# A decoder layer on one core: w_ada sums moved to TensorE, triangular inverses built from 16-blocks, and half the tokens' chunk work begun only with the first FFN

## The chip, the cores and the metric

The kernel runs on one core of a Trainium2 chip. A core has five engines that run side by side, each with its own instructions in a fixed order: TensorE (PE, matmuls, with PEld for its weight loads), VectorE (DVE), ScalarE (ACT), GpSimd (POOL) and SyncE (SP), which here issues nearly all transfers. The metric is the device time of one execution in microseconds (us).

## What is computed

One layer of a conditioned trunk, cut to what matters here (batch 1, 1024 tokens, width 1024, FFN width 2816):

```python
ada = silu(c) @ w_ada + b_ada                    # 1024 -> 6 x 1024
sh_m, sc_m, g_m, sh_f, sc_f, g_f = split(ada, 6)
h = rms_norm(x) * (1 + sc_m) + sh_m
z, u = split(h @ w_in)
y = concat(rwkv7_time_mix(shift(z)), s5_mix(u))  # 8 heads of 64; 32 groups of 16
x = x + g_m * (y @ w_out)
h = rms_norm(x) * (1 + sc_f) + sh_f
x = x + g_f * ((silu(h @ w_gate) * (h @ w_up)) @ w_down)
out = rms_norm(x) * final_gain
```

`rwkv7_time_mix` is a recurrence over tokens. The kernel does it in chunks, and each chunk needs the inverse of a unit triangular matrix.

## The kernel before

**Order.** The program is written as generators that are stepped in turn. `weave` steps several of them in proportion, `LIM(g, n)` takes n steps, `alongside(g, other, n)` runs `g` and takes a step of `other` after every n of its own. This sets priorities; a scheduler then fixes the order of each engine's instructions when the program is built. On the chip each engine takes them strictly in that order.

**Stages.** The start sums parts 0 and 1 of w_ada, normalises x and projects `u`. Then come the S5 work, the projection to z (`pz`) and the chunk work of four token quarters `qt` of 256 tokens. For each quarter `prepare` (tiles `pn`, `pa`, `pw`, `pb`, `pA`, `ak`) builds the chunk matrices, `post` inverts them, `chains` (tiles `p`, `R`, `U`, `ST`) runs the recurrence, and `finishes` (`pd`, `pv`, `pg`, `ld`) normalises, gates and writes y to the DRAM tensor `y_d`. `s5_glu` (`pglu`, `pss`, `zz`) is the S5 gate in four halves. `outproj(half)` reads y (`yt`, split in two parts `yhl`), loads w_out (`wraw`, `wo`) and forms `po`; `norm_f` and `ffn(half)` (`pgate`, `pup`, `pdn`) follow. Half 0 is quarters 0 and 1, half 1 quarters 2 and 3. `late` is the sequence of all the chunk work of quarters 2 and 3, 128 steps.

**w_ada.** `ada_load` (L280) loads 1024 rows of some columns in four tiles `wada`. `ada_acc` (L289) multiplies each of the eight row blocks by a column of silu(c), `cact`, and adds them up in `acc`: on DVE (L295, L297), or, for the first column pair of parts 2 and 3, with ACT multiplying (L299) and POOL adding (L300). `ada_cols` (L303) sums `acc` over partitions with one-column matmuls `pac`. `ada_steps` (L826) does this for two parts, 256 columns at a time: parts 2 and 3 along with the S5 gate and the chains, parts 4 and 5 with the first output projection.

**The inverse.** `solve` (L991) takes 32x32 blocks `LU` from DRAM and eliminates them in 31 steps of two instructions (`stmp` L1006, `XU` L1008), on DVE for quarters 0 and 1, on POOL for quarters 2 and 3. Result and transpose go to the DRAM tensor `x_d` and come back in another layout in `rest` (L1013), where `pG` and `pO` (32x32 tiles of PE) join two 32-blocks to a 64-block.

**The end of the program** (L1415 on) sets where `late` runs: 4 of its steps along with the first steps of the first output projection, 16 more along with the rest of it, and the others in `alongside(late, f0, 2)` (L1442): a step of `f0` after every two of `late`, where `f0` is `norm_f(0)` and `ffn(0)`, 97 steps. After it `f0` runs 28 steps alone, and what is left of it is woven with the second output projection.

## Time and profile before

| | |
|---|---|
| median of 3 runs | 1596.32 us (1594.2 to 1597.29) |
| profiled execution, its own time | 1596.48 us |
| its span in the profile | 1594.8 us |
| mean granted TensorE clock | 0.946 of 2.4 GHz |
| PE / DVE / ACT / POOL busy | 1419.0 / 929.3 / 562.7 / 519.8 us |
| first `pz` / first `pglu` / first `po` | 104.4 / 462.1 / 597.7 us |
| first `pgate` of FFN(0) / first `po` of half 1 / last `po` | 694.2 / 1115.2 / 1203.4 us |

Times in the trace count from the start of the span. An engine's busy share says little by itself, since the kernel passes through stages with different limits: what bounds a stage is read from that stage's windows and waits.

### The profile page before, as it was taken

Reading aid. Unit: us, or ns where it says so; the run is one execution under the profiler, and the core shown is the slowest. Engines: PE = TensorE matmul, PEld = TensorE weight load, DVE = VectorE, ACT = ScalarE, POOL = GpSimd, SP = SyncE. Lnnn points to the kernel's source line nnn. Section 1 sums busy time; section 2 is a strip of 40 time slices with the busy share of each in tenths; the row PEclk is TensorE's granted clock in tenths of the full one; section 3 lists DMA queues with packets and bytes.
Section 4 is the critical chain, followed back from the end, with each engine's and each line's share of the span. In section 5 each row is a group of like instructions: output and inputs, shape, how many; then the busy total and the mean of one; then the engine's idle time right before and its main releaser. Section 6 shows DMA issues by size and latency. Waiting matters only on the chain.

```text
span 1594.8 us, 23226 instructions
## 1 busy us (share of the span) xinstructions
PE 1419.0 (89%) x9167; PEld 1143.2 (72%) x9167; DVE 929.3 (58%) x1618; ACT 562.7 (35%) x909; POOL 519.8 (33%) x480
## 2 busy tenths in 40 slices
...
GB/s 286 139 139 244 264 328 193 164 163 110 154 160 125 126 219 217 59 103 97 61 99 91 88 106 89 84 54 167 177 80 40 151 87 106 92 106 92 98 101 53
DMA packets 255692, 211.80 MB, mean 133 GB/s; under 512 B 71894, under 2 KB 223072, under 8 KB 252000
## 3 DMA queue, kind: packets, MB, share of 16 engines
...
## 4 chain that ended last, share of the span: by engine, by line
PE 51%; DVE 19%; DMA 13%; POOL 5%; ACT 5%; issue 4%; SPq 2%; DVEq 0%; ACTq 0%; POOLq 0%
PE pdn L270 11%; PE pgate L270 10%; PE pup L270 10%; PE pz L270 5%; PE po L1314 4%; DMA wada<-in_w_ada_dram 3%; PE pu L367 2%; DMA rawd<-in_ffn_w_down_dram 2%; PE p L1062 2%; DVE acc L297 2%; POOL stmp L1006 2%; POOL XU L1008 2%; PE pY L762 1%; PE pA L962 1%; DMA LU<-l_d 1%
## 5 line engine op out<-in xcount | busy, mean ns | idle before, releaser
L270 PE MATMUL pdn<-wd,act 128*128 128x512 f32 x1056 | 271.7, 398 | 1.4 <-DVE x L1363 0.5
L270 PE MATMUL pup<-h,hl_up 128*128 128x512 f32 x1056 | 266.5, 395 | 0.2 <-ACT hl_up L131 0.2
L270 PE MATMUL pgate<-h,hl_g 128*128 128x512 f32 x1056 | 262.7, 394 | 2.1 <-ACT hl_g L131 2.0
L270 PEld LDWEIGHTS pdn<-wd,act 128*128 128x128 f32 x1056 | 197.3, 189 | 49.1 <-DVE x L1363 2.4
L270 PEld LDWEIGHTS pgate<-h,hl_g 128*128 128x128 f32 x1056 | 196.6, 188 | 47.2 <-issue 3.2
L270 PEld LDWEIGHTS pup<-h,hl_up 128*128 128x128 f32 x1056 | 197.5, 188 | 43.9 <-issue 2.1
L270 PE MATMUL pz<-hT,hl_z 128*128 128x256 f32 (+1 forms) x1008 | 192.6, 347 | 35.0 <-ACT zo L872 13.5
L1363 DVE TENSOR_TENSOR x<-pdn,x 128x512 f32<-128x512 f32 x176 | 118.8, 688 | 176.6 <-PE pdn L270 176.4
L270 PEld LDWEIGHTS pz<-hT,hl_z 128*128 128x128 f32 x1008 | 159.0, 206 | 64.8 <-ACT zo L872 18.2
L1398 DVE TENSOR_TENSOR rawd<-rawd,gfb 128x1024 f32<-128x1024 f32 x44 | 57.2, 1300 | 111.5 <-DMA rawd<-in_ffn_w_down_dram 89.9
L1314 PE MATMUL po<-wo,yhl 128*128 128x512 f32 x384 | 98.7, 410 | 9.0 <-ACT yhl L1299 4.2
L1314 PEld LDWEIGHTS po<-wo,yhl 128*128 128x128 f32 x384 | 74.4, 197 | 27.3 <-ACT yhl L1299 4.3
L131 ACT CAST wd<-rawd 128x1024 fp32r<-128x1024 f32 x44 | 45.6, 1051 | 122.1 <-DVE rawd L1398 88.8
L131 ACT CAST hl_up<-raw_up 128x1024 fp32r<-128x1024 f32 x44 | 46.2, 1051 | 114.6 <-PE pup L270 105.1
L297 DVE SCALAR_TENSOR_TENSOR acc<-wada,cact,acc 128x256 f32<-128x256 f32 (+1 forms) x112 | 79.0, 710 | 6.9 <-DMA wada<-in_w_ada_dram 5.3
L875 POOL TENSOR_TENSOR zo<-zo,zm 128x512 f32<-128x512 f32 x28 | 44.2, 1580 | 99.5 <-ACT zo L872 86.6
L127 POOL TENSOR_TENSOR hl_g<-raw_g,hl_g 128x1024 fp32r<-128x1024 f32 x19 | 45.5, 2394 | 78.7 <-ACT hl_g L131 78.7
L127 POOL TENSOR_TENSOR yhl<-yt,yhl 128x512 fp32r<-128x512 f32 x16 | 25.0, 1562 | 135.5 <-ACT yhl L1299 130.9
L1392 ACT ACTIVATE sgt<-pgate 128x512 f32<-128x512 f32 x44 | 26.3, 599 | 121.0 <-PE pgate L270 120.0
L127 POOL TENSOR_TENSOR wd<-rawd,wd 128x1024 fp32r<-128x1024 f32 x19 | 49.7, 2616 | 57.4 <-ACT wd L131 57.4
L127 POOL TENSOR_TENSOR wo<-wraw,wo 128x512 fp32r<-128x512 f32 x32 | 44.4, 1393 | 73.6 <-ACT wo L131 73.6
L127 POOL TENSOR_TENSOR hl_up<-raw_up,hl_up 128x1024 fp32r<-128x1024 f32 x19 | 49.9, 2628 | 50.0 <-ACT hl_up L131 50.0
...
## 6 DMA issues: line engine op xcount, KB each, us to landing
...
```

The costliest lines, as they stand in the source:

```text
L127: (eng or G).tensor_tensor(out=out, in0=a, in1=b, op=ALU.subtract)
L131: S.copy(dst[:, 0], src)
L270: PE.matmul(ps, lhsT=lf(a, k), rhs=rf(b, k), start=(n == 0), stop=(n == 3 * kb - 1))
L297: V.scalar_tensor_tensor(out=acc, in0=wt, scalar=cact[:, k:k + 1], in1=acc, op0=ALU.mult, op1=ALU.add)
L367: PE.matmul(pu[hf, b], lhsT=uw[b][:, a_, k, :], rhs=hT[hf, k][:, b_, :], start=(k == 0 and n == 0), stop=(k == 7 and n == 2))
L875: G.tensor_tensor(out=o, in0=o, in1=zm[:, 0:HT], op=ALU.add)
L1006: SOLVE.tensor_tensor(out=t, in0=LU[:, j, j + 1:32].unsqueeze(2).to_broadcast([P, nt, nk]), in1=X[:, j:j + 1, 0:nk].to_broadcast([P, nt, n ...
L1008: SOLVE.tensor_tensor(out=X[:, j + 1:32, 0:nk], in0=X[:, j + 1:32, 0:nk], in1=t, op=ALU.add)
L1062: PE.matmul(ps[r, h], lhsT=a, rhs=b, start=(n == 0), stop=(n == len(ops) - 1))
L1314: PE.matmul(pss[i], lhsT=yh[k][:, a, 128 * i:128 * i + 128], rhs=wo[:, b], start=(k == 4 and n == 0), stop=(k == 3 and n == 2))
L1363: V.tensor_tensor(out=t, in0=ps, in1=t, op=ALU.add)
L1398: V.tensor_tensor(out=raw, in0=raw, in1=gfb, op=ALU.mult)
```

## The change

Three edits. **(A)** `ada_acc` sums on PE: silu(c) stands in column 0 of a zero-filled 32-column block per row block (`cz`), the eight row blocks go to four column groups of the array by turns, each group with its own 32 partitions of the PSUM tile `pada`, and ACT copies the result to `acc`; `ada_cols` then sums over partitions as before. Eight `wada` tiles are held instead of four. **(B)** `solve` inverts 16x16 blocks in 15 steps of two instructions, always on DVE; they are written to the diagonal of 32x32 blocks in `x_d`, whose other places are zeros, in 64-byte pieces. `rest` then forms the 32-block inverses with three rounds of 32x32 tiles on PE, `pH`, `pX` and `pV`, each 64 calls followed by a DVE operation from PSUM, before `pG` and `pO`. **(C)** `late` takes no steps before the FFN: all 128 run in `alongside(late, f0, 2)`.

```diff
@@ -286,18 +296,14 @@
             wts.append(wt)
         return wts
 
-    def ada_acc(pl, wts, n, eng=V):
-
-        acc = pl.tile([P, 128 * n], F32, tag="acc", bufs=2 if n > 2 else 3, name="acc")
+    def ada_acc(pl, wts, n, ps):
+
         for k in range(8):
-            wt = wts[k // 2][:, k % 2, :]
-            if k == 0:
-                V.tensor_scalar_mul(acc, wt, cact[:, 0:1])
-            elif eng is V:
-                V.scalar_tensor_tensor(out=acc, in0=wt, scalar=cact[:, k:k + 1], in1=acc, op0=ALU.mult, op1=ALU.add)
-            else:
-                S.mul(wt, wt, cact[:, k:k + 1])
-                G.tensor_tensor(out=acc, in0=acc, in1=wt, op=ALU.add)
+            g = slice(32 * (k % 4), 32 * (k % 4) + 32)
+            PE.matmul(ps[g, 0:128 * n], lhsT=cz[:, k, :], rhs=wts[k // 2][:, k % 2, :], start=(k < 4), stop=(k > 3),
+                      tile_position=(0, 32 * (k % 4)))
+        acc = pl.tile([P, 128 * n], F32, tag="acc", bufs=2, name="acc")
+        S.copy(acc, ps[:, 0:128 * n])
         return acc
 
     def ada_cols(acc, part, j0, n, ps):
@@ -316,6 +322,8 @@
     param_cols(0, rows0)
     S.activation(cact, col("c", 0, 8), AF.Sigmoid)
     V.tensor_mul(cact, cact, col("c", 0, 8))
+    V.memset(cz, 0.0)
+    V.tensor_copy(cz[:, :, 0], cact)
     def load_x(hf):
         t = sp.tile([P, 4, D], F32, tag="x", bufs=2, name="xt")
         for i in range(4):
@@ -537,7 +545,7 @@
     xts, uw = [load_x(0)], []
     wa = [ada_load(sp, part, 0, 4, 6) for part in range(2)]
     dgs = norm_x(0, xts[0])
-    acs = [ada_acc(sp, w, 4) for w in wa]
+    acs = [ada_acc(sp, w, 4, pst.tile([P, 512], F32, tag="tp", bufs=3, name="pada")) for w in wa]
     transpose_x(xts[0], dgs)
     uw += [load_u(0), load_u(1)]
     xts.append(load_x(1))
@@ -550,7 +558,7 @@
         for b in range(2):
             u_mm(0, k, b)
     dgs = norm_x(1, xts[1])
-    acs = [ada_acc(sp, w, 4) for w in wa]
+    acs = [ada_acc(sp, w, 4, pst.tile([P, 512], F32, tag="tp", bufs=3, name="pada")) for w in wa]
     transpose_x(xts[1], dgs)
     param_cols(1, rows1)
     uw += [load_u(2), load_u(3)]
@@ -674,6 +682,10 @@
                 nc.sync.dma_start(B_d[2 * Q + ri], bs)
                 nc.sync.dma_start(C_d[2 * Q + ri], ca[:, ri, 8 * Q:8 * Q + 8].rearrange("p g n c -> p (g n c)"))
 
+    zero = pp.tile([P, HT], F32, name="zero")
+    G.memset(zero, 0.0)
+    for n in range(2):
+        nc.gpsimd.dma_start(x_d[n], zero)
     s5_params(*s5q)
     pps.close()
 
@@ -823,20 +835,28 @@
             yield
 
 
-    def ada_steps(pl, parts, ps, mix=lambda j: j % 4):
-
-        todo = []
+    def ada_steps(pl, parts, ps):
+
+        loads, todo = [], []
+        def acc():
+            w, part, j = loads.pop(0)
+            todo.append((ada_acc(pl, w, 2, ps("pada")), part, j))
         def cols():
-            acc, part, j = todo.pop(0)
-            ada_cols(acc, part, j, 2, ps("pac2")[:, 0:2])
+            a, part, j = todo.pop(0)
+            ada_cols(a, part, j, 2, ps("pac2")[:, 0:2])
         for part in parts:
             for j in (0, 2, 4, 6):
-                todo.append((ada_acc(pl, ada_load(pl, part, j, 2, 4), 2, V if mix(j) else None), part, j))
-                if len(todo) > 2:
+                loads.append((ada_load(pl, part, j, 2, 8), part, j))
+                if len(todo) > 0:
                     cols()
+                if len(loads) > 1:
+                    acc()
                 yield
-        while todo:
-            cols()
+        while loads or todo:
+            if todo:
+                cols()
+            if loads:
+                acc()
             yield
 
 
@@ -991,35 +1011,49 @@
     def solve(qt):
 
         t_ = lambda nm, sh: RP[0].tile(sh, F32, tag=nm, name=nm)
-        LU, tmp = t_("LU", [P, 32, 32]), t_("stmp", [P, 256])
-        X, VT = (RP[0].tile([P, HT], F32, tag=nm, name=nm) for nm in ("XU", "VT"))
-        X, VT = X.rearrange("p (i k) -> p i k", k=16), VT.rearrange("p (k i) -> p k i", i=32)
-        for o in range(2):
-            nc.sync.dma_start(LU[64 * o:64 * o + 64], l_d[qt][:, 0:2048].rearrange("r (i t) -> r i t", t=64)[:, :, 0:32])
+        LU, tmp, X, VT = t_("LU", [P, 16, 16]), t_("stmp", [P, 64]), t_("X16", [P, 16, 16]), t_("V16", [P, 16, 16])
+        nc.sync.dma_start(LU, l_d[qt].rearrange("r (x n) -> (r x) n", x=2)[:, 0:1024]
+                          .rearrange("r (i t) -> r i t", t=64)[:, :, 0:16])
         G.memset(X, 0.0)
-        for o in range(2):
-            G.memset(X[64 * o:64 * o + 64].rearrange("p i k -> p (i k)")[:, 16 * o:512:33], 1.0)
-        SOLVE = V if qt < 2 else G
-        for j in range(31):
-            nt, nk = 31 - j, j // 2 + 1
+        G.memset(X.rearrange("p i k -> p (i k)")[:, 0:256:17], 1.0)
+        for j in range(15):
+            nt, nk = 15 - j, j + 1
             t = tmp[:, 0:nt * nk].rearrange("p (a b) -> p a b", b=nk)
-            SOLVE.tensor_tensor(out=t, in0=LU[:, j, j + 1:32].unsqueeze(2).to_broadcast([P, nt, nk]),
-                                in1=X[:, j:j + 1, 0:nk].to_broadcast([P, nt, nk]), op=ALU.mult)
-            SOLVE.tensor_tensor(out=X[:, j + 1:32, 0:nk], in0=X[:, j + 1:32, 0:nk], in1=t, op=ALU.add)
-        SOLVE.tensor_copy(VT.rearrange("p k i -> p i k"), X)
-        nc.sync.dma_start(x_d[qt, 0].rearrange("(r n) -> r n", r=P), X.rearrange("p i k -> p (i k)"))
-        nc.sync.dma_start(x_d[qt, 1].rearrange("(r n) -> r n", r=P), VT.rearrange("p k i -> p (k i)"))
+            V.tensor_tensor(out=t, in0=LU[:, j, j + 1:16].unsqueeze(2).to_broadcast([P, nt, nk]),
+                            in1=X[:, j:j + 1, 0:nk].to_broadcast([P, nt, nk]), op=ALU.mult)
+            V.tensor_tensor(out=X[:, j + 1:16, 0:nk], in0=X[:, j + 1:16, 0:nk], in1=t, op=ALU.add)
+        V.tensor_copy(VT.rearrange("p k i -> p i k"), X)
+
+        for n, w in enumerate((X, VT)):
+            d = x_d[n].rearrange("(r s) (i k) -> s r i k", s=2, k=32)
+            for s_ in range(2):
+                nc.sync.dma_start(d[s_, :, :, 16 * s_:16 * s_ + 16], w[s_::2])
 
     def rest(qt):
 
-        XB, VB, GT = (t.rearrange("p (u k) -> p u k", k=32) for t in
-                      [RP[0].tile([P, HT], F32, tag=nm, name=nm) for nm in ("XU", "VT")] + [tr("GT")])
-
-        for o in range(2):
-            src = x_d[qt, :, 32768 * o:32768 * o + 32768]
-            nc.sync.dma_start(XB[:, :, 16 * o:16 * o + 16], src[0].rearrange("(u p k) -> p u k", u=16, k=16))
-            nc.sync.dma_start(VB[o::2], src[1].rearrange("(u p i) -> p u i", u=16, i=32))
+        XB, VB = (t_.rearrange("p (u k) -> p u k", k=32) for t_ in
+                  [RP[0].tile([P, HT], F32, tag=nm, name=nm) for nm in ("XU", "VT")])
+        GT = tr("GT").rearrange("p (u k) -> p u k", k=32)
+        for n, w in enumerate((XB, VB)):
+            nc.sync.dma_start(w, x_d[n].rearrange("(u b) (i k) -> (b i) u k", u=16, k=32))
         aks = [sts[qt, q]["ak"] for q in range(2)]
+
+        def blocks(nm, lf, rf):
+
+            ps = ps_g(nm).rearrange("p (u k) -> p u k", k=32)
+            for u in range(16):
+                for b in range(4):
+                    r = slice(32 * b, 32 * b + 32)
+                    PE.matmul(ps[r, u, :], lhsT=lf(r, u, b), rhs=rf(r, u), start=True, stop=True,
+                              tile_position=(32 * b, 32 * b))
+            return ps
+
+        ps = blocks("pH", lambda r, u, b: aks[u // 8][r, u % 8, 0, 0, 32 * (b % 2):32 * (b % 2) + 32], lambda r, u: XB[r, u, :])
+        V.tensor_tensor(out=GT, in0=ps, in1=mlow.unsqueeze(1).to_broadcast([P, 16, 32]), op=ALU.mult)
+        ps = blocks("pX", lambda r, u, b: VB[r, u, :], lambda r, u: GT[r, u, :])
+        V.tensor_tensor(out=XB, in0=ps, in1=XB, op=ALU.add)
+        ps = blocks("pV", lambda r, u, b: GT[r, u, :], lambda r, u: VB[r, u, :])
+        V.tensor_tensor(out=VB, in0=ps, in1=VB, op=ALU.add)
         ps = ps_g("pG").rearrange("p (u k) -> p u k", k=32)
         for u in range(16):
             ak = aks[u // 8]
@@ -1029,8 +1063,7 @@
                           start=True, stop=True, tile_position=(p0, p0 + 32))
         for h2 in range(2):
             p0 = 64 * h2 + 32
-            S.copy(GT[p0:p0 + 32].rearrange("p u (k o) -> p u o k", o=2),
-                   ps[p0:p0 + 32].rearrange("p u (o k) -> p u o k", o=2))
+            S.copy(GT[p0:p0 + 32], ps[p0:p0 + 32])
         ps = ps_g("pO").rearrange("p (u k) -> p u k", k=32)
         for u in range(16):
             for h2 in range(2):
@@ -1422,11 +1455,11 @@
     op = pool("op", stack=ops)
     solo[0] = True
     o0 = outproj(0, xp0, op, ("s", "p", "A", "G"), lambda: pool("gp", stack=gps, side="right"), "a")
-    weave(seq(c1, finishes(1)), LIM(o0, 4), LIM(late, 4))
+    weave(seq(c1, finishes(1)), LIM(o0, 4))
     ras.close()
     das = ExitStack()
-    adl = ada_steps(pool("adp3", stack=das, side="right"), (4, 5), ps_a, lambda j: True)
-    weave((LIM(late, 16), 2), o0, (LIM(adl, 2), 1))
+    adl = ada_steps(pool("adp3", stack=das, side="right"), (4, 5), ps_a)
+    weave(o0, (LIM(adl, 2), 1))
     for _ in adl:
         pass
     gps.close()
```

(In the rows of order with the change, line numbers are those of the changed file.) What this does to the order of the engines' instructions shows at three places.

PE, from the last `pss` of the S5 gate to the first `po` of the first output projection, before; `pn` is quarter 2's, `pac` belongs to w_ada, `pgb` to the gate's broadcast:

```order
L813 MATMUL pss<-ssum,ones 128x256
L1264 MATMUL pgb<-dgb,ones 128x128 x8
L921 MATMUL pn<-sq,blk 128x512
L306 MATMUL pac_5788<-ones,acc 128x1 x2
L306 MATMUL pac_5809<-ones,acc 128x1 x2
L1314 MATMUL po<-wo,yhl 128x512 x24
L306 MATMUL pac_5830<-ones,acc 128x1 x2
L1314 MATMUL po<-wo,yhl 128x512 x20
```

and with the change, on the same engine at the same place:

```order
L825 MATMUL pss<-ssum,ones 128x256
L1154 MATMUL pg<-gs,g2w 128x256 x2
L303 MATMUL pada<-wada,cz 32x256 x8
L1297 MATMUL pgb<-dgb,ones 128x128 x8
L312 MATMUL pac_6009<-ones,acc 128x1 x2
L303 MATMUL pada<-wada,cz 32x256 x6
L1347 MATMUL po<-wo,yhl 128x512 x8
L303 MATMUL pada<-wada,cz 32x256 x2
L1347 MATMUL po<-wo,yhl 128x512 x16
L312 MATMUL pac_6032<-ones,acc 128x1 x2
```

The `pada` groups now stand between the PE work of that stage, and `pn` of quarter 2 has gone.

PE inside FFN(0), where quarter 2's inverse now stands (before, `pG` and `pO` stood alone among the FFN's matmuls):

```order
L280 MATMUL pup<-h_6386,hl_up 128x512 x3
L996 MATMUL ptm<-ident,bk 128x128 x4
L280 MATMUL pdn<-wd,act 128x512 x3
L1047 MATMUL pH<-XU,ak 32x32 x64
L280 MATMUL pdn<-wd,act 128x512 x9
L280 MATMUL pgate<-h_6256,hl_g 128x512 x3
L280 MATMUL pgate<-h_6274,hl_g 128x512 x3
L280 MATMUL pgate<-h_6291,hl_g 128x512 x3
L280 MATMUL pgate<-h_6307,hl_g 128x512 x2
L996 MATMUL ptm<-ident,vz 128x128 x4
L1047 MATMUL pX<-GT,VT 32x32 x64
L1095 MATMUL p_7196<-tm,ak 64x64 x2
```

The new rounds `pH` and `pX` (and `pV` further on) stand between the FFN's matmuls; the 64 is the count of calls.

PE at the end of `late`: before, the finish of quarter 3 stood among the FFN's matmuls, and so did the second projection's first `po`. With the change:

```order
L280 MATMUL pdn<-wd,act 128x512 x3
L1095 MATMUL p_9518<-ak,tm 64x64 x2
L1095 MATMUL p_9518<-ar,ST 64x64 x2
L1095 MATMUL p_9518<-ak,U 64x64 x2
L1095 MATMUL p_9518<-ak,tm 64x64 x2
L1095 MATMUL p_9518<-ar,ST 64x64 x2
L1095 MATMUL p_9518<-ak,U 64x64 x2
L1132 MATMUL pd<-ar,cen 128x512 x2
L1139 MATMUL pv<-lsq,blk 128x512 x2
L1154 MATMUL pg<-gs,g2w 128x256 x4
L1297 MATMUL pgb<-dgb,ones 128x128 x8
L1347 MATMUL po<-wo,yhl 128x512 x192
```

Behind the last `p` (the chains' tiles) stand `pd`, `pv`, `pg`, `pgb` and all 192 `po`; no matmul of FFN(0) is left for between them. On SP, where the transfers of that place stand:

```order
L269 DMA raw_up<-in_ffn_w_up_dram 128x8x128
L1156 DMA y_d<-ld 128x2x256
L1480 DMA fgb<-in_final_gain_dram 128x1024
L1318 DMA x_4_10492<-in_x_dram 128x1024
L1156 DMA y_d<-ld 128x2x256
L1318 DMA x_5_10494<-in_x_dram 128x1024
L1318 DMA x_6_10496<-in_x_dram 128x1024
L1318 DMA x_7_10498<-in_x_dram 128x1024
L1328 DMA yt<-y_d 128x8x64
L1342 DMA wraw<-in_w_out_dram 128x1x512
```

The reads `yt` stand behind the two writes of `y_d` and the loads of x, and no load of the FFN's weights is left among them.

## Rows read from the trace of the kernel before

**Rows 1.** The page, busy time by engine: us, share of the span, instructions.

```profile
PE 1419.0 (89%) x9167; PEld 1143.2 (72%) x9167; DVE 929.3 (58%) x1618; ACT 562.7 (35%) x909; POOL 519.8 (33%) x480
```

**Rows 2.** Windows by stage: stretch, length, busy us of PE, PEld, DVE, ACT, POOL, clock, DMA share.

```profile
0.00:104.40 104.40, 70.74 (x360) 59.64 (x360) 70.19 (x205) 48.21 (x71) 37.96 (x45) 0.93 0.63 194
230.00:443.50 213.50, 190.50 (x1702) 159.93 (x1703) 160.63 (x360) 89.23 (x170) 48.81 (x46) 0.95 0.55 164
443.50:597.67 154.17, 107.98 (x1218) 83.20 (x1218) 114.01 (x260) 79.00 (x159) 58.09 (x69) 0.80 0.55 159
597.67:694.18 96.51, 78.30 (x435) 61.82 (x435) 68.18 (x110) 28.32 (x52) 38.73 (x27) 0.91 0.45 130
694.18:1203.44 509.26, 498.23 (x3297) 393.86 (x3296) 276.89 (x418) 172.17 (x257) 100.57 (x157) 0.99 0.36 99
```

**Rows 3.** The same view, the end of the GLU stage.

```profile
559.00:572.65 13.65, 8.72 (x53) 8.19 (x53) 13.45 (x33) 6.95 (x13) 2.18 (x3) 0.87 0.45 151
572.65:597.67 25.02, 10.10 (x28) 6.48 (x28) 21.63 (x48) 6.48 (x10) 4.70 (x4) 0.54 0.89 262
```

**Rows 4.** Chain of waits, 455 to 700 us: its shares by line.

```profile
by line: DVE acc L297 11.3%; DMA wada<-in_w_ada_dram 10.7%; PE po L1314 9.2%; issue 6.9%; DMA zz<-z_d 3.9%; DVE zz L820 2.6%; PE pglu L270 2.5%; DMA LU<-l_d 2.4%; DVE acc L295 2.3%; ACT L804 2.1%; DVE zz L805 2.0%; PE p L1062 2.0%; DMA raw_
```

**Rows 5.** Groups of DVE: busy us, mean ns, idle before them.

```profile
L297 DVE SCALAR_TENSOR_TENSOR acc<-wada,cact,acc 128x256 f32<-128x256 f32 x84 | 57.2, 686 | 3.7 <-DMA wada<-in_w_ada_dram 2.4
```

**Rows 6.** Windows, the tile `wada` alone, start of the kernel.

```profile
0.00:104.40 104.40, 25.76 (x32) 0.00 (x0) 0.00 (x0) 0.93 0.63 194
```

**Rows 7.** Timeline of PE near 1094 us: start, duration, line, operation, count.

```profile
1094.36 1.03 PE L1121 MATMUL pg<-gs,g2w 128*128 128x256 f32 x4
```

**Rows 8.** Timeline of PE near 158 us.

```profile
158.06 1.97 PE L635 MATMUL pk<-s5ca,bb 64*16 64x128 f32 x64
```

**Rows 9.** The tile `pss`: durations in ns, first and last start.

```profile
L813 PE MATMUL pss<-ssum,ones x8: 379/379/483, 497.2 to 572.9; 128*128 128x256 f32 x8
```

**Rows 10.** Windows, line 962 (`pA`) alone: PE and weight loads.

```profile
597.67:694.18 96.51, 11.55 (x128) 8.57 (x128) 0.91 0.45 130
694.18:1115.17 420.99, 8.73 (x128) 6.79 (x128) 0.98 0.35 95
```

**Rows 11.** Timeline of PE at the end of the late chains.

```profile
1063.44 0.28 PE L1062 MATMUL p<-ak,U 64*64 64x64 f32 x4
1063.65 1.19 PE L270 MATMUL pup<-h,hl_up 128*128 128x512 f32 x4
1064.69 3.81 PE L270 MATMUL pgate<-h,hl_g 128*128 128x512 f32 x16
```

**Rows 12.** Windows, the tile `stmp` alone: DVE, then POOL.

```profile
330.00:443.50 113.50, 31.90 (x113) 0.00 (x0) 0.97 0.54 146
694.18:1115.17 420.99, 0.00 (x0) 60.04 (x124) 0.98 0.35 95
```

**Rows 13.** Timeline of PE near 740 us.

```profile
740.51 1.20 PE L1028 MATMUL pG<-XU,ak 32*32 32x32 f32 x64 [3.14 <-DMA XU<-x_d]
```

**Rows 14.** Waits of PE, 694.18 to 1115.17: us in all, times, longest.

```profile
PE pG L1028 <- DMA XU<-x_d: 8.9, 2, 5.8
```

**Rows 15.** Timelines of PE, ACT and DVE in the late finish.

```profile
1068.33 1.02 PE L1099 MATMUL pd<-ar,cen 128*128 128x512 f32 x2
...
1082.29 1.28 ACT L1109 ACT_TABLE_LOAD   x1
...
1086.10 0.69 DVE L254 SCALAR_TENSOR_TENSOR lrs<-lsq,lrs 128x512 f32<-128x512 f32 x1
```

**Rows 16.** Timelines of SP and PE around the second output projection's start.

```profile
1105.46 0.38 SPq L1123 DMA_DIRECT2D y_d<-ld  x1
...
1115.17 1.20 PE L1314 MATMUL po<-wo,yhl 128*128 128x512 f32 x4
```

**Rows 17.** Timeline of POOL in the first half of that projection.

```profile
1114.62 1.56 POOL L127 TENSOR_TENSOR yhl<-yt,yhl 128x512 fp32r<-128x512 f32 x1 [123.15 <-ACT yhl L1299]
...
1139.31 2.54 POOL L127 TENSOR_TENSOR wo<-wraw,wo 128x512 fp32r<-128x512 f32 x2
```

10 lines of the change are left out of this document (9 added, 1 removed).

## The prediction

> **What bounds the kernel now.** I read the page first: TensorE (PE) is busy 1419.0 of 1594.8 us [rows 1], so a change pays only where PE idles. The table of windows shows where that is [rows 2]. From the first `pgate` of FFN(0) to the last `po` of the second output projection (694.18 to 1203.44) PE idles 11 us in 509: whatever is added there lengthens the kernel one for one, unless it fills one of the few waits. The opposite holds from 443.50 to 694.18, where the S5 gate (GLU), the w_ada sums of parts 2 to 5 and the first output projection run: PE is busy 108.0 of 154.2 and 78.3 of 96.5 us, so it idles 64.4 of 250.7. I asked which engine it waits for. Between the third and the fourth `pss` (559.00 to 572.65) VectorE (DVE) is busy 13.45 of 13.65 us; from there to the first `po` DVE is busy 21.63 of 25.02 and PE 10.10, at a granted clock of 0.54 [rows 3]. The chain of waits puts 11.3% of 455 to 700 us on the accumulators of line 297 and 10.7% on their loads, before any PE line [rows 4]. So the front of the kernel waits for DVE, and the FFN for PE.
>
> **(A) w_ada on PE.** Removed: 84 DVE instructions of 686 ns on 256 columns [rows 5], the 25.8 us of DVE work on 512 columns at the start [rows 6], and ACT's and POOL's share of parts 2 and 3. Added: eight fp32 matmuls in four column groups per accumulator, one ACT copy, for 4 accumulators of 512 columns and 16 of 256. No row has this shape. The upper bound is no overlap at all: four instructions `pg` of 256 columns on the full array took 1.03 us, 0.26 each [rows 7], and an fp32 matmul is two of them, so 16 instructions or 4.1 us per 256-column accumulator, 66 us for sixteen and 33 for the four wide ones. The lower bound is a quarter of it, four groups side by side. The nearest row is `pk`, also narrow tiles in several groups: 64 instructions of 128 columns in 1.97 us, 31 ns each [rows 8], a quarter of the 0.13 us that half of `pg`'s width would take. I take the quarter: about 1.0 us per 256-column accumulator, 16 in all, and 8 for the wide ones.
>
> - *Start*, 0 to 104 us: DVE sheds the 25.8 us, PE gains 8 of work in a window in which it idles 34 [rows 2]. The first norm and the accumulators share DVE; the loads stay. I take **-3** (-9 to +8).
> - *GLU stage to the first `po`*: the four `pss` start between 497.2 and 572.9, 25.2 us apart on average [rows 9]; the last period is shorter, and its part from 559.00 on, 13.7 us, is DVE's own work [rows 3]. With DVE relieved I let each of the three periods come to 16 or 17: 76 becomes 49, -27. In the 25.0 us from the last `pss` to `po` PE idles 14.9 while DVE is busy 21.6; half of the idle time goes, -8. Sum **-35** (-50 to -25). What holds it there is the load: the DMA share is already 0.89 in that last stretch [rows 3].
> - *First output projection and norm*, 597.67 to 694.18: PE idles 18.2 us [rows 2], and 11.55 us of `pA` of the third quarter stand in it [rows 10]; these leave (C), some 7 us of `pada` and a part of the idle time come and go against each other. **-11.5** (-15 to -5).
>
> The Trainium skill (TensorEngine Tiling (Array Packing), Tiling Modes, Key Properties) says that a change of tiling mode drains TensorE. This kernel's rows show a group of 64x64 tiles at 1063.44 followed by a full-array matmul at 1063.65 [rows 11], 0.21 us on, so a drain costs no more than that here; by the rule alone each of some 20 accumulators would pay two, about 8 us. I leave it within the range.
>
> **(B) The solve from 16-blocks.** Removed: of the DVE solves of quarters 1 and 2, 31.9 us of instructions, about two thirds (30 instructions are left of 62, on at most a quarter of the elements); of the POOL solves of quarters 3 and 4, all 60 us [rows 12], which reappear as some 6 us each on DVE. Added in each quarter: three rounds `pH`, `pX`, `pV`, each 64 calls or 128 PE instructions of 32x32, with a DVE operation of about 0.7 us behind each, and 64-byte pieces to and from x_d. Nearest row: `pG`, 64 instructions of the same tile in 1.20 us [rows 13], 18.7 ns each. So 384 instructions are 7 us a quarter. `pG` uses two tiles in turn, the new rounds four on the diagonal: the lower bound is half, 3.5 us; the upper is the pace of `pk`, 31 ns, 12 us.
>
> The Trainium skill (TensorE: Matmul & The Clock Gate, Part 1, "Wait — 56ns, not 53.3ns?") says that starts never come closer than about 25 ns. The row disagrees with 18.7 on average; by the page the two late quarters would cost 19.2 us, not 14.
>
> - *Quarters 1 and 2*, 230 to 443.5 us: 14 us of PE work, in a window in which PE idles 23 [rows 2], against about 18 us less of DVE work on the chain. **+3** (-5 to +10).
> - *Quarters 3 and 4*, inside FFN(0): PE is full, so **+14** (+7 to +24). In return the two waits of `pG` for XU, 8.9 us [rows 14], mostly go, because the solve is short: **-5** (-11 to 0).
>
> **(C) Late quarters only with the FFN.** Before, 20 of late's 128 steps ran ahead of the FFN. What PE did for them there is `pn`, `pa`, `pw`, `pb` and `pA` of quarter 3. At the FFN's clock `pA` is 8.73 us, by the fourth quarter's instances [rows 10]; the others are some twenty instructions of 256 or 512 columns, at `pg`'s pace 4: **+12.5** us that now stand in the full window.
>
> The other side is the end. FFN(0) has 97 steps. Late takes one per two of its own: 54 before, 64 now; with the fixed 28 that leaves 15 before and 5 now for the second output projection. In the order on PE, the last matmul of FFN(0) now stands ahead of the last three `p` pieces; then `pd`, `pv`, `pg`, `pgb` and 192 `po` in one row, with nothing between. Before, each of these steps had FFN matmuls behind it. On SP the read of y_d (`yt`) stands behind the last write of y_d and three x loads. So the chain from the last `p` to the first `po` is now bare: the last `p` to the write of y_d by its own steps: `pd` 1.0, two ACT passes 1.2, `pv` 1.0, a table load of 1.28 and a root of half that, and 18 DVE instructions for both halves, ten of 0.69 and eight of 0.44, 10.4 us [rows 15]: about 16. The write at 1105.46 to the first `po` at 1115.17: 9.7 [rows 16]. Of these 25.7 us some 6 are PE's own instructions, already there before: **+20**. Then `po`: POOL's `yhl` and `wo` of the first half take from 1114.62 to about 1140.6 [rows 17], 26 us against 96 matmuls of 0.227 = 21.8 (the pace of the sixteen `pgate` from 1064.69 to 1068.33 [rows 11, 15]): **+5**. Between the two halves eight `yo`/`x` operations of 0.69 hold the banks: **+3.5**. The last chain steps, with three matmuls between each, **+2**. Together **+30.5** (+20 to +40).
>
> **Sum.** -3 +3 -35 -11.5 +14 -5 +12.5 +30.5 = +5.5 us. The profiled execution took 1596.48, within 0.2 of the median shown, so the forecast is 1602.
>
> **Rivals.**
> 1. *The front goes to its PE work* (faster). DVE alone held the front, and PE's idle 64.4 us between 443.50 and 694.18 shrink not by 32 but by 50 or more: the two front terms are then -62, the sum -10, 1586. It decides from -43 on in the GLU stage. For it: DVE at 13.45 of 13.65 us. Against: DMA at 0.89, and chains of the first two quarters in the same stage. Chance 0.30.
> 2. *The column groups do not run side by side.* Then the accumulators cost 99 us, 75 more than counted; the idle time takes up about half: 1639. Against it speak `pk` and `pG`. Chance 0.07.
> 3. *The accumulators were not what held the front*: transfers and the chains take the place, the GLU stage gives -10 and not -35: 1627. For it: loads of w_ada hold 10.7% of the chain [rows 4]. Chance 0.12.
>
> **Numbers.** The forecast's case (sum within 15 us of +5.5) has 0.51. About 0.2% (3.2 us) is what a measurement of this kernel can tell from no change. Of the 0.51, 0.07 is faster, 0.12 the same, 0.32 slower. With the rivals: faster 0.37, same 0.12, slower 0.51. The bounds of the terms, taken as independent, give about 23 us to either side of 1602; the rivals lengthen it to 1574 and 1630, and what is left out is rival 2 and the ends of 1 and 3.
>
> **What would show it.** Right: the first `pgate` of FFN(0) comes some 45 us earlier (near 648); from there to the last `po` of the second projection takes 52 us more than 509, with a gap of 20 us or more on PE just ahead of that `po`, its releaser ACT `yhl`; `pH`, `pX`, `pV` at about 2.3 us each. Wrong: a first `pgate` before 635 (rival 1) or after 670 (rival 3); `pada` at 4 us per accumulator (rival 2); no gap ahead of `po`, if the late chains end before the FFN's matmuls are used up.

## The result, and the profile after

1645.33 us median of 4 runs (1635.52 to 1650.38) against 1596.80 (1594.2 to 1603.87): ratio 1.0288, 95% interval 1.0247 to 1.033. The kernel became 48.5 us slower; the forecast was +5.5. The profiled execution took 1650.38 us, at the upper end.

The page of the changed kernel, busy us by engine, to hold against [rows 1]:

```profile
PE 1488.7 (90%) x11023; PEld 1168.3 (71%) x11023; DVE 850.9 (52%) x1499; ACT 555.0 (34%) x898; POOL 426.5 (26%) x329
```

DVE gave up 78 us and POOL 93, PE took on 70. Windows of the changed kernel, cut at its own markers (first and last `pz`, first `po`, first `pgate`, last `po` of half 1), columns as in [rows 2]:

```profile
0.00:105.50 105.50, 87.60 (x423) 59.77 (x423) 47.04 (x173) 51.73 (x75) 38.00 (x50) 1.00 0.66 202
230.00:465.70 235.70, 206.63 (x2441) 174.90 (x2440) 150.97 (x317) 89.62 (x172) 47.50 (x48) 0.91 0.50 150
465.70:606.40 140.70, 110.52 (x1394) 81.07 (x1392) 65.97 (x154) 61.50 (x120) 32.70 (x37) 0.82 0.52 159
606.40:697.90 91.50, 79.71 (x418) 59.49 (x417) 36.91 (x69) 33.83 (x65) 35.01 (x28) 0.89 0.47 137
697.90:1248.70 550.80, 527.76 (x4211) 410.75 (x4209) 310.97 (x523) 175.00 (x269) 36.05 (x31) 0.97 0.33 92
1248.70:1648.70 400.00, 379.99 (x1650) 306.02 (x1648) 167.37 (x217) 107.24 (x150) 159.61 (x67) 0.98 0.30 91
```

The same stretches in both kernels, and what the prediction had for each:

| stretch | before | after | measured | predicted |
|---|---|---|---|---|
| to the first `pz` | 104.4 | 105.5 | +1.1 | -3 |
| to the last `pz` | 338.8 | 360.2 | +21.4 | +3 |
| to the first `po` | 154.5 | 140.7 | -13.8 | -35 |
| to the first `pgate` | 96.5 | 91.5 | -5.0 | -11.5 |
| to the last `po` of half 1 | 509.0 | 550.8 | +41.8 | +52 |
| to the end | 391.6 | 400.0 | +8.4 | 0 |
| sum | | | +53.9 | +5.5 |

The sum is 5 us above the 48.5 of the medians, as the profiled execution is. In the third stretch DVE's work fell from 114.0 to 66.0 us, and the stretch by only 13.8. The part of it that the forecast's -35 was worked out for, from the first `pss` to the first `po`, was 100.5 us before and is 96.4. PE's timeline in the fifth, after the last `p`:

```profile
1164.75 0.28 PE L1095 MATMUL p<-ak,U 64*64 64x64 f32 x4
1165.40 1.13 PE L1132 MATMUL pd<-ar,cen 128*128 128x512 f32 x2 [0.36 <-ACT ar L1114]
1167.20 1.12 PE L1132 MATMUL pd<-ar,cen 128*128 128x512 f32 x2 [0.68 <-ACT ld L1134]
1169.71 2.07 PE L1139 MATMUL pv<-lsq,blk 128*128 128x512 f32 x2 [1.38 <-ACT ld L1134]
1172.66 2.04 PE L1139 MATMUL pv<-lsq,blk 128*128 128x512 f32 x2 [0.88 <-DVE lsq L1140]
1175.48 2.08 PE L1154 MATMUL pg<-gs,g2w 128*128 128x256 f32 x4 [0.78 <-DVE lsq L1140]
1180.80 2.07 PE L1154 MATMUL pg<-gs,g2w 128*128 128x256 f32 x4 [3.24 <-DVE ld L1155]
1183.85 4.75 PE L1297 MATMUL pgb<-dgb,ones 128*128 128x128 f32 x16 [0.98 <-DVE dgb L1296]
1196.91 2.07 PE L1347 MATMUL po<-wo,yhl 128*128 128x512 f32 x4 [8.31 <-ACT wo L131]
```

The chain is bare, as predicted: every step waits for the one before it, 31.9 us from the end of the last `p` to the first `po`. The idle time is 16.6 of them, since from `pv` on PE's own steps take twice as long (`pg` 2.08 us against 1.03 in [rows 7]): the granted clock, 0.51, has fallen to its lower level of 1.2 GHz. The window of it, columns as above:

```profile
1169.00:1197.00 28.00, 13.10 (x29) 7.15 (x29) 11.97 (x28) 5.29 (x9) 0.58 (x1) 0.51 0.52 149
```

The 192 `po` behind take 51.8 us, where 192 matmuls at 0.227 would take 43.6.

### The profile page after: what moved, and what is told of

Same layout as the page of the kernel before. It is cut to its first block, busy times and chain, and to the rows that moved or that the text cites. A ratio compares the mean times of both kernels' runs of the same rounds, so it can differ in the third digit from the quotient of the medians.

```text
span 1648.7 us, 26613 instructions
## 1 busy us (share of the span) xinstructions
PE 1488.7 (90%) x11023; PEld 1168.3 (71%) x11023; DVE 850.9 (52%) x1499; ACT 555.0 (34%) x898; POOL 426.5 (26%) x329
## 4 chain that ended last, share of the span: by engine, by line
PE 71%; DVE 11%; DMA 7%; ACT 4%; issue 4%; SPq 2%; POOL 1%; ACTq 0%; DVEq 0%; POOLq 0%
PE pgate L280 15%; PE pdn L280 14%; PE pup L280 14%; PE pz L280 5%; PE p L1095 4%; PE po L1347 3%; PE pu L375 3%; PE pA L982 2%; PE pY L774 2%; PE pada L303 1%; DMA yt<-y_d 1%; PE ptr L1373 1%; DMA wraw<-in_w_out_dram 1%; PE pglu L280 1%; PE ptr L352 1%
## 5 line engine op out<-in xcount | busy, mean ns | idle before, releaser
L280 PEld LDWEIGHTS pgate<-h,hl_g 128*128 128x128 f32 x1056 | 196.7, 188 | 51.8 <-ACT hl_g L131 4.3
L127 POOL TENSOR_TENSOR yhl<-yt,yhl 128x512 fp32r<-128x512 f32 x16 | 22.6, 1420 | 266.3 <-DMA yt<-y_d 243.5
L891 ACT ACTIVATE zm<-pz,cols 128x256 f32<-128x256 f32 (+1 forms) x42 | 22.9, 544 | 114.5 <-PE pz L280 110.0
L131 ACT CAST hl_g<-raw_g 128x1024 fp32r<-128x1024 f32 x44 | 46.0, 1046 | 43.6 <-DMA raw_g<-in_ffn_w_gate_dram 43.5
```

Source lines behind the costliest of these rows:

```text
L127: (eng or G).tensor_tensor(out=out, in0=a, in1=b, op=ALU.subtract)
L131: S.copy(dst[:, 0], src)
L280: PE.matmul(ps, lhsT=lf(a, k), rhs=rf(b, k), start=(n == 0), stop=(n == 3 * kb - 1))
```

## The experiments

Each is set against the kernel before, unless another is named. A single profile carries its stage boundaries to some 6 us: a kernel whose built order is that of before on PE, ACT and SP (null_mlow_late, below) showed a first `pgate` 5.8 us earlier and the next stretch 5.4 us longer, at the same time. Times are medians of several executions; the ratios and their intervals are estimated from the same executions and are not quotients of these medians. Stage times are from one execution each.

| kernel | median us | ratio, 95% interval |
|---|---|---|
| a_alone: (A) | 1582.47 | 0.9912 (0.9883 to 0.9941) |
| b_alone: (B) | 1634.15 | 1.0222 (1.0185 to 1.0259) |
| c_alone: (C) | 1631.16 | 1.0222 (1.0186 to 1.0259) |
| ab: (A) and (B) | 1613.07 | 1.0103 (1.0072 to 1.0134) |
| after_pad | 1637.14 | 1.0258 (1.0215 to 1.0301) |
| after_3 | 1635.99 | 1.0233 (1.0193 to 1.0272) |
| before_nosum | 1579.47 | 0.9900 (0.9863 to 0.9937) |
| a_steps | 1596.13 | 0.9972 (0.9947 to 0.9997) |
| a_more | 1591.79 | 0.9985 (0.996 to 1.0009) |
| b_late | 1615.48 | 1.0119 (1.0086 to 1.0151) |
| b_early | 1635.06 | 1.0235 (1.0206 to 1.0264) |
| before_null | 1617.40 | 1.0126 (1.0101 to 1.0152) |
| null_mlow | 1609.14 | 1.0057 (1.0037 to 1.0078) |
| null_zero | 1612.01 | 1.0071 (1.0049 to 1.0094) |
| null_mlow_late | 1597.67 | 0.9997 (0.9977 to 1.0017) |
| b_early_ls | 1630.30 | 1.0188 (1.0163 to 1.0212) |
| b_late_ls | 1601.83 | 1.0029 (1.0005 to 1.0053) |
| a_late_ls | 1583.93 | 0.9901 (0.9868 to 0.9934) |

**The parts apart.** a_alone, b_alone and c_alone have one part's hunks of the diff each, ab those of (A) and (B). (C) is this:

```diff
-    weave(seq(c1, finishes(1)), LIM(o0, 4), LIM(late, 4))
+    weave(seq(c1, finishes(1)), LIM(o0, 4))
...
-    weave((LIM(late, 16), 2), o0, (LIM(adl, 2), 1))
+    weave(o0, (LIM(adl, 2), 1))
```

> The kernel before with the w_ada sums on PE alone (edit A); the solve and the late quarters as before. Theory 1 (the front is held by PE's order, the chains of quarters 1 and 2 and the transfers, not by DVE's accumulators): the first pgate within 8 us of 694, the whole 0 to 8 us slower. Theory 2 (DVE held the front, as the forecast had it, and the new rounds of the inverse ate the gain): the first pgate near 650, the whole 30 us faster or more.

> The kernel before with the 16-block inverse alone (edit B). Theory 1: the z stage 8 to 14 us longer, the rounds pH, pX, pV 3.7 us a quarter inside the FFN against 9 us of waits for XU that go, together 5 to 15 us slower. Theory 2: 30 us slower or more, nearly all of it ahead of the first pglu, since B has to eat what A gives.

> The kernel before with the late quarters begun only with the FFN (edit C alone). Both theories: the first pgate some 10 us earlier, the stretch from there to the last po 30 to 40 us longer with a bare chain ahead of the second projection, 20 to 30 us slower in all. If the bare end costs little: within 5 us of before.

> The changed kernel with edit C undone: w_ada on PE and the 16-block inverse, 20 steps of the late quarters ahead of the FFN as before. Theory 1: A and B add up to 8 to 22 us slower than before, and C is worth 25 to 35 us of the change's 49. Theory 2: within 5 us of before, C the whole of the loss.

(A) alone gains 14 us, (B) alone costs some 35 (31 on top of A), (C) alone some 35 (32 on top of A and B). The expectation of a_alone held in neither of its theories, and c_alone lost more than its 20 to 30. c_alone spends 551.4 us from the first `pgate` to the last `po` of half 1 (before 509.0), +42.4 where the forecast's two terms for (C) there make 43.0, and gets to that `pgate` 14.0 us sooner: the trade loses. (A)'s gain does not stand where the forecast had it. From the last `pz` to the first `po` a_alone needs 148.3 us against 154.5, -6; the last `pz` itself comes 13 us earlier. Its first `pY<-X,Tt`, a matmul of the S5 work, stands at 228.7 instead of 239.6; where DVE still sums at the start, in a_steps below, it stands at 238.4. In a_alone's order this `pY` also stands ahead of `pz` pieces that it stood behind before, so relief of DVE and order are not told apart. a_alone's row of this instruction:

```profile
L760 PE MATMUL pY<-X,Tt x64: 270/377/580, 228.7 to 377.9; 128*128 128x128 f32 x64
```

With (B) beside it the same instruction stands at 239.7 (ab), and that gain is gone; in a_late_ls below, with the old inverse in the early quarters and the set-up late, it stands at 228.7 again.

**Was the GLU stage held by the sums?** before_nosum keeps the loads of w_ada and leaves out seven of the eight row blocks of each sum in parts 2 to 5, so those sums are not computed. a_steps is a_alone with the sums of parts 0 and 1, at the start, on DVE as before. a_more is a_alone with more late steps ahead of the FFN.

```diff
-        for k in range(8):
+        for k in range(8 if n > 2 else 1):
```

a_steps, against a_alone, `ada_acc` in it summing on DVE where n is 4:

```diff
-    acs = [ada_acc(sp, w, 4, pst.tile([P, 512], F32, tag="tp", bufs=3, name="pada")) for w in wa]
+    acs = [ada_acc(sp, w, 4, None) for w in wa]
```

a_more, against a_alone:

```diff
-    weave((LIM(late, 16), 2), o0, (LIM(adl, 2), 1))
+    weave((LIM(late, 32), 3), o0, (LIM(adl, 2), 1))
```

> The kernel before with the sums of w_ada's parts 2 to 5 left out: of the eight row blocks only the first is scaled, the loads and the one-column matmuls stay, so the gates and the second modulation are not the reference's. It takes 66 us from DVE and 24 from POOL and adds nothing to PE. Theory 1 (the accumulators did not hold the S5 gate's stage): the first pglu to the first po still takes 120 to 132 us of 135.6, the whole at most 15 us faster. Theory 2 (they did, and pada's own work ate the gain): 100 us or less, the whole 35 us faster.

> The w_ada sums on TensorE for parts 2 to 5 only; those of parts 0 and 1, at the start, on VectorE as before. The sums on TensorE in all parts gave -14 us. If that gain comes from the GLU stage and the first output projection (parts 2 to 5 overlap them): -8 to -14, first pgate 12 to 20 earlier than 694.2, with most of it between 443 and 694. If it comes from the start: 0 to -3, the last pz near 443 rather than near 430. If it comes out of the order of the schedule at large: a result outside both, and a last pz that moves though nothing in that stage has changed.

> The sums on TensorE alone, with the weave of the first output projection changed to 32 steps of the late quarters, three to one, in place of 16 steps, two to one: the opposite direction of part C. If PE's idle time ahead of the FFN still has room (some 55 us between the last pz and the first pgate): 3 to 10 us below the kernel with the sums alone, the first pgate up to 8 later, the last po 8 to 15 earlier than it less that. If the front is as full as its chains allow: the first pgate moves out by as much as the FFN gains, the same time within 3 us, or slower.

The window of before_nosum from its last `pz` to its first `po`:

```profile
439.20:585.60 146.40, 105.16 (x1221) 82.52 (x1219) 88.64 (x213) 67.39 (x131) 35.94 (x41) 0.79 0.55 164
```

DVE is busy 89 of 146 us, and PE still idles 41: with nearly no sums the stretch is 8 us shorter than before, not 35. And the 8 us lie ahead of the first `pss`. From `pss` to `pss`, before (the part behind the last one is in [rows 3]), then from `pss` to `pss` and to the first `po` in before_nosum, columns as in [rows 2]:

```profile
497.15:524.21 27.06, 23.65 (x270) 18.82 (x268) 21.62 (x51) 14.36 (x33) 7.80 (x8) 0.87 0.43 131
524.21:557.04 32.83, 25.47 (x223) 18.11 (x221) 30.26 (x63) 20.93 (x38) 15.59 (x16) 0.84 0.45 137
557.04:572.65 15.61, 9.32 (x56) 8.38 (x54) 15.41 (x37) 8.88 (x18) 2.18 (x3) 0.89 0.39 132
```
```profile
484.31:510.80 26.49, 23.41 (x299) 19.29 (x297) 20.00 (x51) 16.18 (x30) 5.28 (x4) 0.87 0.57 176
510.80:537.04 26.24, 20.47 (x250) 17.70 (x248) 19.01 (x45) 8.40 (x16) 6.64 (x5) 0.81 0.27 83
537.04:556.75 19.71, 14.37 (x73) 10.25 (x72) 13.62 (x29) 18.09 (x32) 2.43 (x4) 0.93 0.18 53
556.75:585.60 28.85, 12.56 (x32) 7.82 (x32) 19.54 (x41) 6.93 (x10) 4.62 (x4) 0.50 0.78 244
```

From the first `pss` to the first `po` it is 100.5 us before and 101.3 without the sums (101.1 in a_alone): nothing is gained where the forecast had -35. In all before_nosum is 16 us faster, spread over its stretches. What waits there now is spread over the chains and the gate (from 439 to 700 us: `pgb` for `dgb` 6.8 us, `ptm` for `tm` 5.7, `pac` for `sg` 5.4), at a clock of 0.79. No run takes out the loads of w_ada: whether they hold the last window, at a DMA share of 0.78, is not shown. The first stretch of [rows 3], where DVE was full, was 13.7 us of 154.

a_steps gains 0.28%, some 4.5 us by its ratio (1.5 by the medians), so of (A)'s 14 some 10 to 12 come with the sums at the start. (A) makes another order too, with two instructions for `cz` at the start; no run has those alone, so part of the 14 may be order. a_more reaches the first `pgate` 43 us later than a_alone and runs from there to the last `po` in 464.9 instead of 512.1; the end then takes 407.6 instead of 391.1, because steps of FFN(0) that no longer ran beside `late` went behind that `po`. In all it is 9 us slower than a_alone: the front has no free room for late work, and (C)'s opposite does not pay either.

**128 bytes.** In after_pad `mlow` takes 256 bytes a partition in place of 128, which moves the tiles allocated behind it.

```diff
-    mlow = const.tile([P, 32], F32, name="mlow")
+    mlow = const.tile([P, 64], F32, name="mlow")[:, 0:32]
```

> The changed kernel with one number altered: the 128-byte constant mlow takes 256 bytes per partition, so that all tiles behind it lie 128 bytes further on. In every run with B the matmuls of the second FFN start 233.3 ns apart, without B 226.7. Theory (the 128-byte shift against the tiles at the other end of the memory does it): 226.7 again, the stretch from the last po to the end 391 us and not 400, the whole 7 to 10 us faster than the changed kernel. Rival (something else of B, its instructions or its transfers): 233.3 as before, no difference.

Timeline of PE in FFN(1), first the changed kernel, then after_pad:

```profile
1407.89 3.89 PE L280 MATMUL pgate<-h,hl_g 128*128 128x512 f32 x16
1411.63 2.96 PE L280 MATMUL pdn<-wd,act 128*128 128x512 f32 x12
```
```profile
1402.24 3.79 PE L280 MATMUL pgate<-h,hl_g 128*128 128x512 f32 x16
1405.87 2.88 PE L280 MATMUL pdn<-wd,act 128*128 128x512 f32 x12
```

From one start to the next sixteen matmuls take 3.74 and 3.63 us: 234 and 227 ns each. The last stretch falls from 400.0 to 390.9 us, the whole by 8.2 in the medians, though there the two intervals overlap. In the first FFN, runs of eight and more matmuls keep a pace of some 228 ns in both: which operands the shift touches, and how, is open. The slower pace stands in all four kernels with the 128-byte tile (the changed one, b_alone, ab, after_3) and in none without it.

**The bare end.** after_3 lets `late` run three steps, not two, to one of `f0`, so that steps of FFN(0) are left for the late chain's end.

```diff
-    alongside(late, f0, 2)
+    alongside(late, f0, 3)
```

> The changed kernel with one step of the first FFN per three steps of late instead of two, so that some 27 of its 97 steps are left for the second projection. Theory (C costs what the bare end costs): the wait ahead of the first po of the second projection falls under 5 us, po stands among FFN matmuls, 20 to 30 us faster than the changed kernel. Rival (the late chains, packed more tightly, now wait for their own results on PE): within 8 us of the changed kernel, with waits of p and pG instead.

PE no longer waits ahead of the first `po`, as the theory had it, but the kernel gains less than its 20 to 30 us. From the first `pgate` to the last `po` it takes 511.9 us, 38.9 less; but the end takes 425.6, 25.6 more, since the FFN work that would fill the gap was taken from it. Net 9 us by the medians: the order of `late` can be mended only in part with this number.

**Where (B) loses.** b_late has the new inverse in quarters 3 and 4 only, b_early in 1 and 2 only, before_null in none: it has just the set-up, unused. All keep `mlow` in 256 bytes, and their new solve has its blocks inside the old `LU` tile, where the changed kernel has tiles of their own. Which solve is taken, in b_late (`qt < 2` and `solve_e` the old one there; in b_early the other way round), and the set-up:

```diff
+    def solve(qt):
+        return solve_e(qt) if qt < 2 else solve_l(qt)
...
+    V.memset(mlow, 0.0)
+    for b in range(4):
+        G.affine_select(...)
...
+    zero = pp.tile([P, HT], F32, name="zero")
+    G.memset(zero, 0.0)
+    for n in range(2):
+        nc.gpsimd.dma_start(x_d[n], zero)
```

> The kernel before with the 16-block inverse in quarters 3 and 4 alone, the old solve in 1 and 2, and mlow at 256 bytes. Theory (B's price lies in the z stage, where its rounds queue behind pz, and in the shifted tiles): within 5 us of before, 7.4 us of rounds against 9 of waits for XU. Rival (the rounds and their waits cost inside the FFN): 10 us slower or more.

> The new solve in the first two quarters only, the old one in the last two, mlow in 256 bytes. Theory R (rounds and waits of the new solve cost the S5 stage its time): first pgate at 705 or later, 10 to 25 us slower than before, with PE waits on s5ca, kb or U of 4 us and more ahead of the last pz. Theory S (set-up re-orders the schedule): as slow as the kernel with the set-up alone, within 5 us. A third theory, N (the loss of the changed solve lies in the late quarters inside the FFN): first pgate within 5 us of 694.2 and at most 4 us slower than before.

> The kernel before, with its own solve in all four quarters; added are only the set-up instructions that the new solve brings: mlow (a memset and four affine_selects, kept in 256 bytes, so that the addresses behind it keep their place modulo 256) and the zero tile with its two stores to an otherwise unused buffer. The result is the same. Theory S (the S5 stage of the changed solve is late because these instructions re-order what the list scheduler emits from the first stages on): 8 to 15 us slower than before, first pgate at 702 to 710, the last pz at 449 or later. Theory R (the rounds and the waits of the new solve itself cost the S5 stage its time): within 4 us of before, first pgate within 4 of 694.2, last pz within 5 of 443.2.

The set-up alone costs 20 us, more than its theory's 8 to 15 and as much as b_late, so that b_late's 19 are no price of its rounds; the early quarters add 17.7. Theory S and theory R both hold a part.

**What in the set-up costs it.** null_mlow has the five instructions of `mlow` alone, at the start; null_zero the zero tile and its stores alone. null_mlow_late has `mlow` at the same address, its five instructions written just ahead of the first output projection (`solo[0] = True`). The `_ls` kernels ("late set-up") take b_early and b_late with the set-up moved down to ahead of its first use (zero tile of 256 columns, four stores); a_late_ls is (A) on b_late_ls. The places, in null_mlow_late, b_early_ls and b_late_ls:

```diff
+    V.memset(mlow, 0.0)
...
     solo[0] = True
```
```diff
+    V.memset(mlow, 0.0)
...
     weave((post(0), 1), (prepare(1), 2), LIM(zg, 1))
```
```diff
+    V.memset(mlow, 0.0)
...
     ras.close()
     das = ExitStack()
```

> The kernel before with five unused instructions more: mlow's memset on VectorE and its four affine_selects on POOL, where the change has them, at the start of the program. As built, they shift the order of the first stages (PE's first transposes stand in another order from its second entry on). Theory S (another order of the whole program is what the set-up costs): 8 to 20 slower than before, as the kernel with the whole set-up was. Rival Z (the fill of the zero tile and its two stores on POOL's queue are what costs): within 3 us of before.

> The same tile at the same address and the same five instructions, but written in the program behind the chunk work of the first half, so that nothing else is placed after them by the scheduler's priorities: the built order is that of before on PE, ACT and SP, with one entry more on VectorE and one group of four on POOL. Theory S: the same as before within 3 us. Rival W (the work or the address of the tile itself is what costs): as slow as with the instructions at the start.

> The kernel before with the zero tile, its memset and two stores alone, where the change has them (ahead of the S5 parameters). The built order is that of before up to PE's 91st entry and differs after. Theory S: some change of either sign, 3 to 20 us. Rival M (mlow at the start is what costs): within 3 us.

> The new solve in quarters 1 and 2 only, as before, but with the set-up written just ahead of the first inverse instead of at the start, so that the order of the first 235 PE entries is that of the kernel before. Theory R2 (the rounds on PE and their waits cost the S5 stage some 17 us by themselves): first pgate at 708 to 716, 14 to 20 slower than before. Theory S2 (most of the loss was the order, from the set-up on): within 6 us of before, first pgate 692 to 700.

> The new inverse in quarters 3 and 4 only, with its set-up written behind the chunk work of the first half: PE's order is that of before for its first 893 entries. With the set-up at the start this kernel was 19 us slower than before, the set-up alone 20. Theory S (the order made by the set-up was the loss): first pz to first pss as in before within 2 us, and the same time as before within 5 us, since the rounds cost 7 us of PE and the two waits of pG, 8.9 us, go. Rival L (the rounds inside the FFN cost what they add): 7 to 12 slower.

> The w_ada sums on TensorE together with the kernel just above (new inverse in quarters 3 and 4, set-up late). If the parts add: the w_ada sums' -14 and what the late quarters cost alone, thus 1582 give or take 5, first pgate near 673. If the order decides: anywhere from -20 to +10, and the difference does not stand where the changed instructions are.

`mlow` at the start costs 9 us, the zero fill 11; `mlow`'s instructions late cost nothing (0.9997). So for `mlow` it is their place in the program, and with it the order that the scheduler builds, not their work nor the address; nor do they hold the start up (first `pz` at 106.0 and 105.6). The zero fill was not run late by itself; b_late_ls has both late and costs some 4 us with its new rounds. One thing that the order changes shows in the S5 stage. The window 255 to 270 us of null_mlow, null_mlow_late, b_early_ls and the changed kernel, in turn:

```profile
255.00:270.00 15.00, 15.00 (x73) 12.87 (x73) 12.30 (x23) 5.61 (x9) 6.66 (x4) 0.71 0.55 176
```
```profile
255.00:270.00 15.00, 15.00 (x104) 12.05 (x104) 12.00 (x23) 7.92 (x12) 4.73 (x4) 1.00 0.68 222
```
```profile
255.00:270.00 15.00, 14.63 (x74) 11.93 (x73) 11.32 (x24) 6.09 (x9) 1.95 (x3) 0.73 0.55 173
```
```profile
255.00:270.00 15.00, 12.35 (x52) 10.40 (x52) 11.87 (x22) 2.69 (x4) 2.82 (x4) 0.56 0.49 154
```

In the first two PE is full, yet gets through 73 instructions or 104 in 15 us, as the granted clock is 0.71 or 1.00, partly at its lower level of 1.2 GHz; in the changed kernel PE also idles 2.7 us. It is 1.00 in before, null_mlow_late, b_late_ls and a_alone, and 0.70 to 0.73 in null_mlow, null_zero, before_null and b_early_ls; but it is 0.77 in a_late_ls too, which is as fast as a_alone. In b_early_ls a wait of PE precedes it that before does not have at that place:

```profile
253.35 0.79 PE L764 MATMUL pY<-L,CA 64*128 64x128 f32 x2 [6.70 <-DVE L L741]
```

null_mlow and before wait alike just there (3.60 and 3.59 us for `zo`), and only null_mlow loses the clock; so the wait does not explain all. These two and null_mlow_late run the same instructions there, in the same order. The same 24 `pz` in null_mlow, then in null_mlow_late:

```profile
261.80 5.49 PE L277 MATMUL pz<-hT,hl_z 128*128 128x256 f32 x24
```
```profile
258.72 3.14 PE L271 MATMUL pz<-hT,hl_z 128*128 128x256 f32 x24
```

From the first `pY` to the first `pA` behind it null_mlow needs 29.6 us and before 25.8: with like waits, the lower clock costs some 4 us here, a part of the 9. The profiles put the rest into the fifth stretch, first `pgate` to last `po`: 519.4 us in null_mlow, 519.8 in null_zero, 520.3 in before_null, 522.2 in b_early_ls, against 509.0 before and 514.4 in null_mlow_late, with the same matmuls and the old late quarters in all of them. What lengthens it is open.

b_early_ls still loses 30.6 us, well above the 14 to 20 of its theory R2: the early quarters cost by themselves, wherever the set-up stands. From the first to the last `pz` it needs 361.4 us, 22.6 more; from 330 us to the last `pz`:

```profile
330.00:466.30 136.30, 125.29 (x1763) 108.28 (x1761) 84.97 (x206) 44.74 (x96) 23.62 (x24) 0.91 0.46 123
```

The rounds are 7.7 us of PE's 125 (the rows of `pH`, `pX`, `pV` by form, 3.9, 2.3 and 1.5), and the clock is 0.91 against 0.97 before. What the rounds do beyond their work shows in the second quarter, before and then in b_early_ls:

```profile
455.66 1.92 PE L1028 MATMUL pG<-XU,ak 32*32 32x32 f32 x64 [3.84 <-DMA XU<-x_d]
```
```profile
449.41 0.31 PE L1030 MATMUL pH<-XU,ak 32*32 32x32 f32 x12 [1.91 <-DMA XU<-x_d]
449.65 4.60 PE L272 MATMUL pz<-hT,hl_z 128*128 128x256 f32 x24
454.19 0.99 PE L1030 MATMUL pH<-XU,ak 32*32 32x32 f32 x92
455.25 3.14 PE L272 MATMUL pz<-hT,hl_z 128*128 128x256 f32 x24
458.31 0.39 PE L1030 MATMUL pH<-XU,ak 32*32 32x32 f32 x24
...
467.83 1.15 PE L1030 MATMUL pV<-VT,GT 32*32 32x32 f32 x113
...
471.81 1.20 PE L1045 MATMUL pG<-XU,ak 32*32 32x32 f32 x64
```

The rounds stand in PE's order between `pz` pieces of 24, and each round has to wait for the one before it. So 4.7 us of rounds take 22.4 us from the first `pH` to `pG`: the solve ends 5 us sooner than before and `pG` starts 16 us later. In the first quarter the solve ends 33 us sooner (372 against 405 us) and `pG` starts 1 us sooner (411.5 against 412.5). The last `pY` still stands only 5 us later than before, the last `pz` 23 us. The prices of the parts do not add up (20, 18, 4 and 8 for set-up, early, late, address make 50, b_alone has 35): each kernel is also another order.

Late quarters with the set-up out of the way cost some 4 us (b_late_ls, 3.5 by the medians), and (A) with them is as fast as (A) alone. No kernel that computes the whole beats a_alone; it beats before by 14 us and the changed kernel by 63.

## Why the prediction was wrong

The sign of the likeliest case was right and its size 43 us too small; the time lies above the range.

- **What bounds the kernel.** Right for the FFN: what was added there lengthened it. Wrong for the front: "the front of the kernel waits for DVE" was read from 13.7 us in which DVE is full and from a chain of which 11.3% is the sums, and was carried over to the 100 us from the first `pss` to the first `po`.
- **The step that failed: the GLU stage, -35.** From the first `pss` to the first `po` it measured -4.1 in the changed kernel, +0.6 with (A) alone and +0.8 with hardly a sum left. Over the longer stretch from the last `pz` these are -13.8, -6.2 and -8.1, and c_alone, with all the sums on DVE, has -10.6 there. Each period from `pss` to `pss` was let fall from 25 us to 16. But 15.6 is what the last period took with DVE full; the first two took 27.1 and 32.8 with DVE busy for 21.6 and 30.3 of them, and without sums they take 26.5 and 26.2. What else in them is late was not asked. That the accumulators did not hold the front was rival 3 (chance given: 0.12); that transfers and chains take their place, its other half, no run has tested.
- **The S5 stage, +3, fails as well.** Measured +21.4. Only PE work against DVE work was counted, and PE's was less than counted: 9.6 us for 14. That each round stands in PE's order behind `pz`, so that three rounds are three waits on the chain, that the early quarters by themselves cost 30 (b_early_ls), and that a few instructions at the program's start rebuild the order, was in no term. With the stage behind it that is +7.6 for -32: 40 of the 48 us missed.
- **Start, -3.** The first `pz` did not move, and PE's new work there was 17 us, not 8 [rows 2]: `pada` came four instructions at a time, at 1.05 or 1.92 us each time. With (A) alone a gain shows later, as a first `pY` 11 us sooner; with (B) beside it, it is gone.
- **First output projection, -11.5.** Measured -5.0, and +2.0 in c_alone: `pA` leaving it does not shorten it. The front as a whole does get 14.0 us shorter in c_alone, but ahead of `po`.
- **Column groups side by side.** Right: 16 instructions of `pada` start within 1.0 us where they stand together. Rival 2 fell. Where they do not, they cost more: the sixteen accumulators of 256 columns took 23.2 us of PE in all, not 16.

```profile
643.97 1.07 PE L303 MATMUL pada<-wada,cz 128*32 128x256 f32 x16
```

- **Rounds in the FFN, +14, and `pG`'s waits, -5.** Mis-sized: line 1047's `pH` alone, over both late quarters, columns as in [rows 10] with DVE added:

```profile
697.90:1150.00 452.10, 2.79 (x256) 2.46 (x256) 1.38 (x2) 1.00 0.33 90
```

  2.79 us for 256, and 2.57 each for `pX` and `pV`: 4.0 us a quarter, near the lower bound of 3.5. No wait of `pG` for XU is left in that stretch (before 8.9). That makes -1 of the +9; b_late_ls, with nothing but these late quarters and a set-up, measures some 4, and the difference is not accounted for. The Trainium skill (TensorE: Matmul & The Clock Gate, Part 1, "Wait — 56ns, not 53.3ns?") has starts no closer than about 25 ns; the row has 10.9 ns on average for four tiles in turn, and the row decides.
- **The bare end, +30.5.** Right in place and size. (C) alone adds 42.4 us to the stretch, for 43.0 from this term and the +12.5 together. In the changed kernel the chain was 31.9 us for 25.7, of which PE's own 15.3 (at the lower clock, which no term had) for some 6, and 51.8 us for 192 `po` against 43.6 is +8.2 for the +8.5 of pacing and banks. The releaser of `po` was ACT `wo`, not `yhl`. The stretch came to +41.8 instead of +52, as the rounds and waits were 10 cheaper.
- **The end, 0.** Measured +8.4, all of it the 128 bytes of `mlow`: after_pad's last stretch is that of before. No rival had it.
- **Still open:** what drops the clock near 255 us in one order and not in another, how the 30 us of the early quarters divide between the rounds' waits in PE's queue, the order and the clock, and what holds the front in the place of the sums.
